# Stick-breaking attention: the causal mask inside the running product, and contiguous state transfers

## The chip, the cores and the metric

One core of one Trainium2 chip runs the whole step. The metric is the device time of one execution in microseconds; the median of several executions is compared. The profile is of one execution, recorded by the hardware. Its five engines are called here PE (TensorE, with its weight loads as PEld), DVE (VectorE), ACT (ScalarE), POOL (GpSimd) and SP (SyncE, which issues nearly all transfers).

## The reference

One inference step of a two-layer decoder, for 256 prompt rows and 8 sample rows (264 columns in all) that share the weights. Layer 0 mixes block-sparse attention with a gated unit, layer 1 mixes stick-breaking attention with a causal pooling mixer; each layer ends in a gated feed-forward net with a width-3 causal convolution. The change concerns layer 1:

```python
z = jnp.einsum('bqhd,bkhd->bhqk', qh, k).astype(jnp.float32) * scale
before = kpos[None, :] < pos[:, None]
log_keep = jnp.where(before, jax.nn.log_sigmoid(-z), 0.0)
later = lax.cumsum(log_keep, axis=3, reverse=True) - log_keep
w = jnp.where(before, jnp.exp(jax.nn.log_sigmoid(z) + later), 0.0)
return jnp.einsum('bhqk,bkhd->bqhd', w.astype(v.dtype), v)
```

So w is sigmoid(z) times the product of sigmoid(-z) over the later keys that come before the query, and zero from the query's own key on. The pooling mixer takes sums over windows of 2, 4, 8 and 16 rows; each sample brings its last 15 rows as state and hands back the last 15 of the new 16. The feed-forward net brings and hands back two state rows for each sample and layer in the same way.

## The kernel before

Activations lie transposed: features on the 128 partitions, the 264 rows along the free dimension. Every weight matrix is cut into 128x128 blocks, streamed in the order of use: a chunk `raw` of 16 blocks (1 MB) is loaded by SP into one of three buffers, tiles of 8 blocks are split into a high half `wh` (ACT, L300) and a low half `wl` (DVE, L301), and PE does three matmuls per block (L325 to L327). `split` runs three tiles ahead, so the DVE split of a chunk's second half is what frees its buffer for the chunk three later.

`run` goes through one phase (in0, out0, ff0, dn0, in1, out1, ff1, dn1) block by block. Between blocks it calls hooks: `blk(b, f)` puts a piece of attention or pooling work behind block b. In the phases in and out the order of PE's instructions is kept as written. A helper, `late`, issues a transfer on SP and keeps it at the place in SP's order where it was written; a plain `nc.sync.dma_start` may be moved by the scheduler. SP works strictly in order, so a transfer that waits holds up those behind it. The transfers on SP also share eight completion semaphores in turn, so each waits until the eighth before it has landed.

In the in1 phase of layer 1 the hooks are, in order: the pooling sums (`pool_sum`), the loads of the cached values V (two at every eighth block from 40), the pooling products `pm`, at 72 the sample scores (`zs_score`), from 80 on four groups `z_qk(t)` for the prompt (two heads each), at 82 the transposes pP of the samples' result (`zs_tr`), the transposes pt of the groups (`z_tr`), and at 100 and 108 the two groups of products with V, `pv_l`, which need all V loads of their samples.

A group `z_qk(t)` first writes a mask of -1e30 above and on the diagonal into both PSUM banks with a bf16 matmul of the identity and `maskb1` (L971), then adds the products of q and k: columns 0 to 127 for the first 128 queries, columns 128 to 383 for the others. `stick` (L958) then takes sigmoid(-z) of all 384 columns as `keep` and sigmoid(z) as `w` on ACT, runs the products backwards over the keys with one scan on DVE (L964; `edge` holds a 1 at column 127 at which the product starts anew), and multiplies (L965). The same function serves the samples, without a mask.

Three transfers of state have short pieces: `PALL` takes the pooling state, 15 of every 16 values, 32 times on each partition (60 bytes a piece, 4096 pieces); `out_pools` stores it shifted by one, 4096 pieces again; the two stores `out_cs` take 8 values for each of 22 blocks on each partition (32 bytes, 2816 pieces each).

Of the kernel before, what the change touches and what calls it, by code (L numbers as in the profile page):

```python
# [9 lines left out]
F32 = mybir.dt.float32  # L10
F32R = mybir.dt.float32r
BF16 = mybir.dt.bfloat16
I32 = mybir.dt.int32
AF = mybir.ActivationFunctionType
ALU = mybir.AluOpType
# [3 lines left out]
P = 128  # L19
D = 1024  # L20
KD = D // P
SEQ = 256
NS = 8
T = SEQ + NS
HD = 64
NH = 8
PAST = 256
# [4 lines left out]
NF = DFF // P  # L32
# [11 lines left out]
NEG = -1e30  # L44
SCALE = HD ** -0.5
POOLW = (2, 4, 8, 16)
NST = 15
# [33 lines left out]
_NB = sum(len(o) for _, o in _PHASES)  # L81
# [68 lines left out]
_NVEC = _vec_layout()  # L150
# [3 lines left out]
def _consts():  # L154
    f = np.float32
    parts = []

    def add(name, a):
        full = np.zeros((P, a.shape[1]), f)
        full[: a.shape[0]] = a  # L160
        _CST[name] = (sum(x.shape[1] for x in parts), a.shape[1])
        parts.append(full)

    half = 8
    inv = (f(500000.0) ** (-(np.arange(half, dtype=f) * f(2.0) / f(16)))).astype(f)
    pos = np.concatenate([np.arange(SEQ), np.full(NS, PAST)]).astype(f)
    ang = (pos[None, :] * inv[:, None]).astype(f)
    c, s = np.cos(ang.astype(np.float64)).astype(f), np.sin(ang.astype(np.float64)).astype(f)
    C, S = np.ones((P, T), f), np.zeros((P, T), f)
    for b in (0, 64):  # L170
        C[b:b + 8], C[b + 8:b + 16] = c, c
        S[b:b + 8], S[b + 8:b + 16] = -s, s
    r = np.arange(P)
    global _ROPE
    _ROPE = np.ascontiguousarray(np.concatenate([C, S], 1))
    add("ident", np.eye(P, dtype=f))
    add("m0", np.where(r[None, :] > r[:, None], f(NEG), f(0)).astype(f))
    add("m1", np.where(r[None, :] >= r[:, None], f(NEG), f(0)).astype(f))
    g32, h32 = r // 32, r % 32
    used = (h32 < 2 * NS)[:, None]  # L180
    ts = np.arange(4 * NS)[None, :]
    add("sm", (used & (g32[:, None] == ts // NS) & (h32[:, None] // 2 == ts % NS)).astype(f))
    add("hs", (used & (h32[:, None] % 2 == r[None, :] // HD)).astype(f))
    add("icnt", np.concatenate([np.tile((f(1) / np.minimum(np.arange(16) + 1, w).astype(f))[None, :], (P, 1)) for w in POOLW], 1))
    return np.ascontiguousarray(np.concatenate(parts, 1))


_CST_ARR = _consts()

_INS = [  # L190
    ("w", ((_NB - 16) * P * P,)), ("xw", (P * (KD + 16 * P + KD * T),)), ("x", (P, KD * T)), ("vec", (P, _NVEC)), ("cst", _CST_ARR.shape), ("rope", (P, 2 * T)),
    ("kt0", (NPHYS, P, 512)), ("vp0", (NPHYS, P, 512)), ("kt1", (NPHYS, P, 512)), ("vp1", (NPHYS, P, 512)),
    ("cstate", (P, 2 * NF * 2 * NS)), ("pstate", (P, 4 * NS * NST)),
    ("sguw", (P, 512)), ("sgub", (P, 512)), ("poolw", (P, 512)),
]
_OUTS = [
    ("y", (KD, P, T)), ("k0", (P, 4, T)), ("v0", (P, 4, T)), ("bvn", (P, 4, NS)),
    ("k1", (P, 4, T)), ("v1", (P, 4, T)), ("poolp", (P, 4, NST)), ("pools", (P, 4, NS, NST)),
    ("cv0", (P, NF, 10)), ("cv1", (P, NF, 10)), ("cs0", (P, NF, NS)), ("cs1", (P, NF, NS)),
]  # L200

# [2 lines left out]
def tile_decoder_step(ctx: ExitStack, tc: tile.TileContext, a):  # L204
    nc = tc.nc
    v, s, g = nc.vector, nc.scalar, nc.gpsimd
# [14 lines left out]
    pe = TensorE()  # L221

    con = ctx.enter_context(tc.tile_pool(name="con", bufs=1))
# [3 lines left out]
    pp = ctx.enter_context(tc.tile_pool(name="pp", bufs=4))  # L227
# [4 lines left out]
    def f4(name, shape=(P, 4, T), dt=F32):  # L232
        return up.tile(list(shape), dt, tag="u", name=name)
# [11 lines left out]
    VEC = con.tile([P, _NVEC], F32, name="VEC")  # L245
    CST = con.tile([P, _CST_ARR.shape[1]], F32, name="CST")
    PT = con.tile([1, NS * NPG], I32, name="PT")
    CSTATE = con.tile([P, 2, NF, 2, NS], F32, name="CSTATE")
    C0 = con.tile([P, 2, NF, NS], F32, name="C0")
    PALL = con.tile([P, 4, NS, 16], F32, name="PALL")  # L250

# [8 lines left out]
    def cst(n):  # L260
        o, w = _CST[n]
        return CST[:, o:o + w]
# [11 lines left out]
    def late(dst, src):  # L274
        tc.keep_in_program_order(nc.sync.dma_start(dst, src))
# [69 lines left out]
    first, o = [], 0  # L345
    for i in range(len(_FIRST)):
        g_, w_, x_ = _first_cols(i)
        n = g_ + w_ + x_
        r = f4(f"xw{i}", (P, n))
# [181 lines left out]
    def conv_prep(l):  # L531
        cw = vec("cw")
        w = lambda i: cw[:, (l * 3 + i) * NF:(l * 3 + i + 1) * NF].unsqueeze(2).to_broadcast([P, NF, NS])
        t = sm.tile([P, NF, NS], F32, tag="cprep", name=f"cprep{l}", bufs=1)
        g.tensor_tensor(C0[:, l], CSTATE[:, l, :, 0, :], w(0), ALU.mult)
        g.tensor_tensor(t, CSTATE[:, l, :, 1, :], w(1), ALU.mult)
        g.tensor_tensor(C0[:, l], C0[:, l], t, ALU.add)
        nc.sync.dma_start(a[f"cs{l}"], CSTATE[:, l, :, 1, :])

    def ffn(l, xg, R, down_evac, hooks=None):  # L540
        cw, cb = vec("cw"), vec("cb")
# [106 lines left out]
    rope = f4("rope")  # L648
# [9 lines left out]
            in0_evac(m, o)  # L658

    maskb0 = con.tile([P, 384], BF16, name="maskb0")  # L660
    maskb1 = con.tile([P, 384], BF16, name="maskb1")
    identb = con.tile([P, P], BF16, name="identb")

    def two(x):

        return x.rearrange("p (b k) -> p b k", k=P)[:, 0:3:2, :]

    def masks():
        for mk, c in ((maskb0, "m0"), (maskb1, "m1")):
            for b in (0, SEQ):  # L670
                tc.keep_in_program_order(s.activation(mk[:, b:b + P], cst(c), AF.Copy))
        tc.keep_in_program_order(s.activation(identb, ident, AF.Copy))

    q4, k4, v4 = f4("q4"), f4("k4"), f4("v4")
# [187 lines left out]
    blk = lambda b, f, *x: hk.at(b / 8 - 1, f, *x)  # L862
# [51 lines left out]
        blk(8, s_av, t)  # L914


    late(CSTATE, a["cstate"].rearrange("p (l j i s) -> p l j i s", l=2, j=NF, i=2))
    for l in range(2):
        conv_prep(l)

# [11 lines left out]
    ffn(0, xg, R, evac, hk)  # L932


    late(PALL[:, :, :, 0:NST], a["pstate"].rearrange("p (g s i) -> p g s i", g=4, s=NS))
    xg = xg1
    q4, k4, v4 = f4("q4b"), f4("k4b"), f4("v4b")
    vt = f4("vt1", (P, 2, 512))
# [9 lines left out]
    def norm1():  # L948
        nonlocal R
        R = nrm1.finish()  # L950
        sigmoid_set()


    edge = f4("edge", (P, 384))
    g.memset(edge, 0.0)
    g.memset(edge[:, P - 1:P], 1.0)

    def stick(w, z, n, e, name):  # L958


        keep = pp.tile([P, n], F32, tag="keep", name=f"keep_{name}", bufs=2)
        s.activation(keep, z, AF.Sigmoid, scale=-1.0)
        s.activation(w, z, AF.Sigmoid)
        v.tensor_tensor_scan(keep[:, ::-1], keep[:, ::-1], e[:, ::-1], 1.0, ALU.mult, ALU.max)  # L964
        v.tensor_tensor(w[:, :n - 1], w[:, :n - 1], keep[:, 1:], ALU.mult)  # L965

    def z_qk(t):
        pss = [at(f"Z1_{2 * t + i}") for i in range(2)]
        hd = [(q4[b:b + 64, t, :], k4[b:b + 64, t, :]) for b in (0, 64)]
        for ps in pss:  # L970
            pe.matmul(two(ps), identb, two(maskb1), start=True, stop=False, skip_group_check=True)  # L971
        for ps, (qh, kh) in zip(pss, hd):
            pe.matmul(ps[:, 0:P], qh[:, 0:P], kh[:, 0:P], start=False, stop=False, skip_group_check=True)
        for ps, (qh, kh) in zip(pss, hd):
            pe.matmul(ps[:, P:384], qh[:, P:SEQ], kh[:, 0:SEQ], start=False, stop=True, skip_group_check=True)
        for i, ps in enumerate(pss):
            w = st1["w", 2 * t + i] = pp.tile([P, 384], F32, tag="p", name=f"w1_{2 * t + i}")
            stick(w, ps[:, :384], 384, edge, 2 * t + i)
        if t == 3:
            lnexp()  # L980

# [14 lines left out]
    def zs_score():  # L996
        ps = at("sc1")
        sample_score(ps, sample_q(qz1, q4, v.tensor_copy), ktiles, range(NS))
        w = st1["zs"] = pp.tile([P, PAST], F32, tag="p", name="zs")
        stick(w, ps[:, :PAST], PAST, edge[:, P:], "s")  # L1000

    def zs_tr():
        pP = mmb("pP1")
# [65 lines left out]
        blk(b, z_qk, t)  # L1069
    for t, b in enumerate((91, 104, 116)):  # L1070
        blk(b, z_tr, t)
    blk(100, lambda: nc.sync.dma_start(a["k1"], k4))
    for i, b in enumerate((62, 66, 70, 76)):
        blk(b, pool_mix, i)
    for t, b in enumerate((110, 118, 126)):
# [1 line left out]
    for i, b in enumerate((100, 108)):  # L1077
        blk(b, sample_av_of(st1, PZ, vtiles, i, "l1"))
    run(orders["in1"], pick(xg), in1_evac, hk)
    nc.sync.dma_start(a["v1"], v4)  # L1080
    hk = Hooks()
    blk(1, zs_out)
    blk(2, z_tr, 3)
    blk(6, lambda: v_pair(vt, v4[:, 3, :], 3, "v1"))
    for t in range(4):
        blk(9, z_av, t)
    nc.sync.dma_start(a["poolp"], plp)
    nc.sync.dma_start(a["pools"], PALL[:, :, :, 1:16])

    xg, nrm, evac = residual(vec("f1"), "f1")  # L1090
    run(orders["out1"], pick([catA, catB]), evac, hk)
# [6 lines left out]
    for i, (m, e) in enumerate(YD):  # L1098
        x = X[:, m:e, :]
# [4 lines left out]
def _lay(inp):  # L1104
# [14 lines left out]
        "vec": np.concatenate([vecs[n] for n in _VEC], 1),  # L1119
        "cst": _CST_ARR,  # L1120
        "rope": _ROPE,
        "kt0": kt(f["cache_l0_kv"]), "vp0": f["cache_l0_kv"][:, :, 1].reshape(NPHYS, P, 512),
        "kt1": kt(f["cache_l1_kv"]), "vp1": f["cache_l1_kv"][:, :, 1].reshape(NPHYS, P, 512),
        "pt": f["page_table"].reshape(1, NS * NPG),
        "cstate": f["state_ffn_conv"].reshape(2, NS, 2, NF, P).transpose(4, 0, 3, 2, 1).reshape(P, -1),
        "pstate": f["state_l1_pool"].reshape(NS, NST, 4, P).transpose(3, 2, 0, 1).reshape(P, -1),
        "sguw": f["l0_sgu_w"].transpose(2, 0, 1).reshape(P, 512),
        "sgub": np.tile(f["l0_sgu_b"].reshape(1, 512), (P, 1)),
        "poolw": f["l1_pool_w"].transpose(1, 0, 2).reshape(P, 512),
# [40 lines left out]
```

## Time and profile before

| | us |
|---|---|
| median of three executions | 611.6 (610.9 to 612.25) |
| profiled execution, its own time | 612.44 |
| its span, first to last instruction | 610.3 |
| PE busy in the span | 593.2 (97%) |
| DVE / ACT / POOL busy | 417.4 / 343.8 / 66.7 |
| mean granted PE clock | 0.994 of full speed |

The span is what the profile shows; 2.14 us of the execution lie around it. Matmuls overlap in the pipeline: a single one is recorded with 284 ns, but they start 0.12 us apart, so their pace is read from stretches and not from single lengths. "a <- b" in a wait means that a stood still until b was done.

### The profile page before, as it was taken

How to read it: one execution, taken by the hardware profiler on the slowest of the kernel's cores; microseconds unless marked ns; L12 is line 12 of the kernel's file. 1: busy time of each engine (PE TensorE's matmuls, PEld its weight loads, DVE VectorE, ACT ScalarE, POOL GpSimd, SP SyncE). 2: the span in 40 equal slices, each digit the busy share in tenths (PEclk: the TensorE clock that was granted, in tenths of full speed). 3: DMA queues.
4: the chain of work that ended last, by engine and by line, in shares of the span. 5: the costliest groups of instructions: out<-in, count | busy, mean ns of one | idle time of the engine just before them, and what ended most of it. 6: DMA issues, size and time to landing. Idle time of an engine off the chain costs nothing.

```text
span 610.3 us, 12279 instructions
## 1 busy us (share of the span) xinstructions
PE 593.2 (97%) x4908; PEld 573.3 (94%) x4908; DVE 417.4 (68%) x711; ACT 343.8 (56%) x607; POOL 66.7 (11%) x83
## 2 busy tenths in 40 slices
PE   8999999999999999999999799999999999999994
PEld 7988879999999999999999588999999999999994
DVE  6899566879776766655559276597986766754442
ACT  7757755576655555544454256566665555555441
POOL 4100002341000000011110000033300000001120
PEclk9999999999999999999999999999999999999998
DMA  8998936544654554894579992445365454564502
GB/s 324 347 396 293 333 123 173 200 147 139 213 202 164 182 205 150 333 333 166 201 178 86 262 356 106 169 154 198 133 214 177 169 207 158 189 209 154 199 1 71
DMA packets 41258, 122.23 MB, mean 200 GB/s; under 512 B 17138, under 2 KB 18546, under 8 KB 29810
## 3 DMA queue, kind: packets, MB, share of 16 engines
q1 hardware_dynamic: 40368, 120.25, 60.0%
q10 hardware_dynamic: 834, 1.20, 0.6%
q8 instruction: 38, 0.62, 0.4%
q14 instruction: 18, 0.15, 0.1%
HBM read 117.50 MB, written 3.94 MB: 199 GB/s over the span
## 4 chain that ended last, share of the span: by engine, by line
PE 71%; DVE 3%; DMA 2%; issue 1%; ACT 1%; POOL 0%; DVEq 0%; SPq 0%; ACTq 0%
PE mm L216 68%; DMA raw<-in_w 2%; DVE xn_l L386 1%; DVE wl L301 1%; PE pv_l L216 1%; PE Z L216 1%; PE pav L216 0%; DVE wk L565 0%; PE pt L219 0%; DVE X L1100 0%; DVE wk L566 0%; ACT wh L300 0%; POOL wk L576 0%; DVE wk L561 0%; PE vtp_v L219 0%
## 5 line engine op out<-in xcount | busy, mean ns | idle before, releaser
L301 DVE TENSOR_TENSOR wl<-raw,wh 128x1024 fp32r<-128x1024 f32 x179 | 220.4, 1231 | 132.7 <-ACT wh L300 130.8
L300 ACT ACTIVATE wh<-raw 128x1024 fp32r<-128x1024 f32 x179 | 189.6, 1060 | 184.4 <-PE mm L216 164.0
L216 PE MATMUL mm<-xn_h,wh 128*128 128x264 f32 x544 | 154.7, 284 | 0.0
L216 PE MATMUL mm<-xn_l,wh 128*128 128x264 f32 x544 | 154.5, 284 | 0.0
L216 PE MATMUL mm<-xn_h,wl 128*128 128x264 f32 x544 | 153.4, 282 | 0.0
L216 PEld LDWEIGHTS mm<-xn_h,wh 128*128 128x128 f32 x544 | 102.2, 188 | 0.2 <-ACT cvo L568 0.2
L216 PEld LDWEIGHTS mm<-xn_l,wh 128*128 128x128 f32 x544 | 102.2, 188 | 0.0
L216 PEld LDWEIGHTS mm<-xn_h,wl 128*128 128x128 f32 x544 | 102.2, 188 | 0.0
L216 PE MATMUL mm<-a_l,wh 128*128 128x264 f32 x352 | 99.8, 284 | 0.0
L216 PE MATMUL mm<-a_h,wh 128*128 128x264 f32 x352 | 99.7, 284 | 0.0
L216 PE MATMUL mm<-a_h,wl 128*128 128x264 f32 x352 | 99.3, 282 | 0.0
L216 PEld LDWEIGHTS mm<-a_l,wh 128*128 128x128 f32 x352 | 66.1, 188 | 0.0
L216 PEld LDWEIGHTS mm<-a_h,wl 128*128 128x128 f32 x352 | 66.1, 188 | 0.0
L216 PEld LDWEIGHTS mm<-a_h,wh 128*128 128x128 f32 x352 | 66.0, 188 | 0.0
L216 PE MATMUL mm<-xg_h,wh 128*128 128x264 f32 x160 | 48.2, 301 | 1.3 <-ACT xg_h L385 1.3
L216 PE MATMUL mm<-xg_f_h,wh 128*128 128x264 f32 x160 | 46.0, 288 | 2.0 <-DVE wk L575 2.0
L216 PE MATMUL mm<-xg_l,wh 128*128 128x264 f32 x160 | 46.2, 289 | 0.0
L216 PE MATMUL mm<-xg_h,wl 128*128 128x264 f32 x160 | 46.1, 288 | 0.0
L216 PE MATMUL mm<-xg_f_l,wh 128*128 128x264 f32 x160 | 45.4, 284 | 0.0
L216 PE MATMUL mm<-xg_f_h,wl 128*128 128x264 f32 x160 | 45.1, 282 | 0.0
L216 PE MATMUL mm<-xg_n_h,wh 128*128 128x264 f32 x128 | 39.2, 307 | 0.0
L216 PE MATMUL mm<-xg_n_l,wh 128*128 128x264 f32 x128 | 36.9, 288 | 0.0
(249 smaller groups left out, 1055.5 us busy)
## 6 DMA issues: line engine op xcount, KB each, us to landing
raw<-in_w SPq DMA_DIRECT2D x89, 1024.0 KB, 4.9
K<-in_kt SPq DMA_DIRECT2D x32, 256.0 KB, 6.1
V<-in_vp SPq DMA_DIRECT2D x32, 256.0 KB, 7.2
raw<-in_w SPq DMA_DIRECT2D x4, 512.0 KB, 5.8
X<-in_x SPq DMA_DIRECT2D x4, 264.0 KB
xw<-in_xw SPq DMA_DIRECT2D x2, 388.0 KB, 5.6
out_k<-k SPq DMA_DIRECT2D x1, 528.0 KB
out_v<-v SPq DMA_DIRECT2D x1, 528.0 KB
```

What stands on the lines that cost most here:

```text
L216: return self.keep(nc.tensor.matmul(*x, **k))
L300: s.activation(h, src, AF.Copy)
L301: v.tensor_tensor(l, src, h.bitcast(F32), ALU.subtract)
L386: j = v.scalar_tensor_tensor(l, src, gain, h.bitcast(F32), ALU.mult, ALU.subtract)
```

## The change

The mask products and `maskb1` go. The first Z product now starts the bank. `keep` moves to two fixed tiles of 385 columns, in which columns 128 and 384 hold zero; ACT fills columns 1 to 127 and 129 to 383 in two instructions. The scan runs over columns 383 to 1 from 0, and `edge`, now an input loaded by SP, has a 1 at each row's own key, the first that is masked: as the scan takes the larger of the product and the edge, it stays zero beyond that key and starts with 1 there. The samples get a function of their own, `stick_all`, with one zero column of `edge` broadcast.

PALL is loaded and stored in full, 16 of 16 values (the first is dropped on the host), and CSTATE is laid out so that its load and the stores `out_cs` are one piece per row. The stores of the pooling state, k1 and v1 are written with `late` at blocks 84, 112 and (in out1) 12.

```diff
+    _EDGE = np.zeros((P, 384), f)
+    _EDGE[r[1:], r[1:]], _EDGE[r, 2 * P + r] = 1, 1
...
-    add("m1", np.where(r[None, :] >= r[:, None], f(NEG), f(0)).astype(f))
...
-    ("cstate", (P, 2 * NF * 2 * NS)), ("pstate", (P, 4 * NS * NST)),
+    ("cstate", (P, 2 * NF * 2 * NS)), ("pstate", (P, 4 * NS * 16)),
...
-    CSTATE = con.tile([P, 2, NF, 2, NS], F32, name="CSTATE")
+    CSTATE = con.tile([P, 2, 2, NF, NS], F32, name="CSTATE")
...
-        nc.sync.dma_start(a[f"cs{l}"], CSTATE[:, l, :, 1, :])
+        nc.sync.dma_start(a[f"cs{l}"], CSTATE[:, l, 1])
...
-        for mk, c in ((maskb0, "m0"), (maskb1, "m1")):
-            for b in (0, SEQ):
-                tc.keep_in_program_order(s.activation(mk[:, b:b + P], cst(c), AF.Copy))
+        for b in (0, SEQ):
+            tc.keep_in_program_order(s.activation(maskb0[:, b:b + P], cst("m0"), AF.Copy))
...
-    late(PALL[:, :, :, 0:NST], a["pstate"].rearrange("p (g s i) -> p g s i", g=4, s=NS))
+    late(PALL, a["pstate"].rearrange("p (g s i) -> p g s i", g=4, s=NS))
...
     edge = f4("edge", (P, 384))
-    g.memset(edge, 0.0)
-    g.memset(edge[:, P - 1:P], 1.0)
-
-    def stick(w, z, n, e, name):
-        keep = pp.tile([P, n], F32, tag="keep", name=f"keep_{name}", bufs=2)
+    late(edge, a["edge"])
+
+    keeps = [con.tile([P, 385], F32, name=f"keep{i}") for i in range(2)]
+    for z in keeps:
+        g.memset(z[:, P:P + 1], 0.0)
+        g.memset(z[:, 384:385], 0.0)
+
+    def stick(w, z, t):
+        n, keep = 384, keeps[t % 2]
+        for a0, a1 in ((1, P), (P + 1, n)):
+            s.activation(keep[:, a0:a1], z[:, a0:a1], AF.Sigmoid, scale=-1.0)
+        s.activation(w, z, AF.Sigmoid)
+        v.tensor_tensor_scan(keep[:, 1:n][:, ::-1], keep[:, 1:n][:, ::-1], edge[:, 1:][:, ::-1], 0.0, ALU.mult, ALU.max)
+        v.tensor_tensor(w, w, keep[:, 1:], ALU.mult)
+
+    def stick_all(w, z):
+        n = PAST
+        keep = pp.tile([P, n], F32, tag="p", name="keep_s")
         s.activation(keep, z, AF.Sigmoid, scale=-1.0)
         s.activation(w, z, AF.Sigmoid)
-        v.tensor_tensor_scan(keep[:, ::-1], keep[:, ::-1], e[:, ::-1], 1.0, ALU.mult, ALU.max)
+        v.tensor_tensor_scan(keep[:, ::-1], keep[:, ::-1], edge[:, P:P + 1].to_broadcast([P, n]), 1.0, ALU.mult, ALU.max)
         v.tensor_tensor(w[:, :n - 1], w[:, :n - 1], keep[:, 1:], ALU.mult)
...
-        for ps in pss:
-            pe.matmul(two(ps), identb, two(maskb1), start=True, stop=False, skip_group_check=True)
         for ps, (qh, kh) in zip(pss, hd):
-            pe.matmul(ps[:, 0:P], qh[:, 0:P], kh[:, 0:P], start=False, stop=False, skip_group_check=True)
+            pe.matmul(ps[:, 0:P], qh[:, 0:P], kh[:, 0:P], start=True, stop=False, skip_group_check=True)
...
-    blk(100, lambda: nc.sync.dma_start(a["k1"], k4))
+    blk(84, late, a["poolp"], plp)
+    blk(84, late, a["pools"], PALL)
+    blk(112, late, a["k1"], k4)
...
-    nc.sync.dma_start(a["v1"], v4)
...
-    nc.sync.dma_start(a["poolp"], plp)
-    nc.sync.dma_start(a["pools"], PALL[:, :, :, 1:16])
+    blk(12, late, a["v1"], v4)
```

More of the change, by code (lines that the diff above doesn't have):

```diff
@@ L173, in _consts @@
     r = np.arange(P)
-    global _ROPE
+    global _ROPE, _EDGE
+    _EDGE = np.zeros((P, 384), f)
+    _EDGE[r[1:], r[1:]], _EDGE[r, 2 * P + r] = 1, 1
     _ROPE = np.ascontiguousarray(np.concatenate([C, S], 1))
@@ L190 @@
 _INS = [
-    ("w", ((_NB - 16) * P * P,)), ("xw", (P * (KD + 16 * P + KD * T),)), ("x", (P, KD * T)), ("vec", (P, _NVEC)), ("cst", _CST_ARR.shape), ("rope", (P, 2 * T)),
+    ("w", ((_NB - 16) * P * P,)), ("xw", (P * (KD + 16 * P + KD * T),)), ("x", (P, KD * T)), ("vec", (P, _NVEC)), ("cst", _CST_ARR.shape), ("rope", (P, 2 * T)), ("edge", (P, 384)),
     ("kt0", (NPHYS, P, 512)), ("vp0", (NPHYS, P, 512)), ("kt1", (NPHYS, P, 512)), ("vp1", (NPHYS, P, 512)),
-    ("cstate", (P, 2 * NF * 2 * NS)), ("pstate", (P, 4 * NS * NST)),
+    ("cstate", (P, 2 * NF * 2 * NS)), ("pstate", (P, 4 * NS * 16)),
     ("sguw", (P, 512)), ("sgub", (P, 512)), ("poolw", (P, 512)),
@@ L197 @@
     ("y", (KD, P, T)), ("k0", (P, 4, T)), ("v0", (P, 4, T)), ("bvn", (P, 4, NS)),
-    ("k1", (P, 4, T)), ("v1", (P, 4, T)), ("poolp", (P, 4, NST)), ("pools", (P, 4, NS, NST)),
+    ("k1", (P, 4, T)), ("v1", (P, 4, T)), ("poolp", (P, 4, NST)), ("pools", (P, 4, NS, 16)),
     ("cv0", (P, NF, 10)), ("cv1", (P, NF, 10)), ("cs0", (P, NF, NS)), ("cs1", (P, NF, NS)),
@@ L534, in conv_prep @@
         t = sm.tile([P, NF, NS], F32, tag="cprep", name=f"cprep{l}", bufs=1)
-        g.tensor_tensor(C0[:, l], CSTATE[:, l, :, 0, :], w(0), ALU.mult)
-        g.tensor_tensor(t, CSTATE[:, l, :, 1, :], w(1), ALU.mult)
+        g.tensor_tensor(C0[:, l], CSTATE[:, l, 0], w(0), ALU.mult)
+        g.tensor_tensor(t, CSTATE[:, l, 1], w(1), ALU.mult)
         g.tensor_tensor(C0[:, l], C0[:, l], t, ALU.add)
-        nc.sync.dma_start(a[f"cs{l}"], CSTATE[:, l, :, 1, :])
+        nc.sync.dma_start(a[f"cs{l}"], CSTATE[:, l, 1])
     def ffn(l, xg, R, down_evac, hooks=None):
@@ L660, in tile_decoder_step @@
     maskb0 = con.tile([P, 384], BF16, name="maskb0")
-    maskb1 = con.tile([P, 384], BF16, name="maskb1")
     identb = con.tile([P, P], BF16, name="identb")
@@ L914, in tile_decoder_step @@
         blk(8, s_av, t)
-    late(CSTATE, a["cstate"].rearrange("p (l j i s) -> p l j i s", l=2, j=NF, i=2))
+    late(CSTATE, a["cstate"].rearrange("p (l i j s) -> p l i j s", l=2, i=2, j=NF))
     for l in range(2):
@@ L977, in z_qk @@
             w = st1["w", 2 * t + i] = pp.tile([P, 384], F32, tag="p", name=f"w1_{2 * t + i}")
-            stick(w, ps[:, :384], 384, edge, 2 * t + i)
+            stick(w, ps[:, :384], 2 * t + i)
         if t == 3:
@@ L999, in zs_score @@
         w = st1["zs"] = pp.tile([P, PAST], F32, tag="p", name="zs")
-        stick(w, ps[:, :PAST], PAST, edge[:, P:], "s")
+        stick_all(w, ps[:, :PAST])
     def zs_tr():
@@ L1121, in _lay @@
         "rope": _ROPE,
+        "edge": _EDGE,
         "kt0": kt(f["cache_l0_kv"]), "vp0": f["cache_l0_kv"][:, :, 1].reshape(NPHYS, P, 512),
@@ L1124, in _lay @@
         "pt": f["page_table"].reshape(1, NS * NPG),
-        "cstate": f["state_ffn_conv"].reshape(2, NS, 2, NF, P).transpose(4, 0, 3, 2, 1).reshape(P, -1),
-        "pstate": f["state_l1_pool"].reshape(NS, NST, 4, P).transpose(3, 2, 0, 1).reshape(P, -1),
+        "cstate": f["state_ffn_conv"].reshape(2, NS, 2, NF, P).transpose(4, 0, 2, 3, 1).reshape(P, -1),
+        "pstate": np.pad(f["state_l1_pool"].reshape(NS, NST, 4, P).transpose(3, 2, 0, 1), ((0, 0), (0, 0), (0, 0), (0, 1))).reshape(P, -1),
         "sguw": f["l0_sgu_w"].transpose(2, 0, 1).reshape(P, 512),
@@ L1160 @@
     poolp = o["poolp"].transpose(2, 1, 0).reshape(1, NST, 512)
-    pools = o["pools"].transpose(2, 3, 1, 0).reshape(NS, NST, 512)
+    pools = o["pools"][..., 1:].transpose(2, 3, 1, 0).reshape(NS, NST, 512)
     cvp, cvs = [], []
```

## The prediction

> **What bounds the kernel now.** I read the page first, then the windows, the chain that ended last, the waits, and the SyncE queue's timeline around the one place where TensorE stands still.
>
> ```profile
> span 610.3 us, 12279 instructions
> ...
> PE 593.2 (97%) x4908; PEld 573.3 (94%) x4908; DVE 417.4 (68%) x711; ACT 343.8 (56%) x607; POOL 66.7 (11%) x83
> ...
> DMA packets 41258, 122.23 MB, mean 200 GB/s; under 512 B 17138, under 2 KB 18546, under 8 KB 29810
> ```
>
> TensorE is busy for 593.2 of 610.3 us, so an edit can pay in two ways only: by taking matmuls away, or by closing one of the gaps that make up the other 17.1 us. In windows of 2 us (PE busy, PEld, DVE, ACT, POOL, granted clock, DMA share, GB/s) the largest gap stands out:
>
> ```profile
> 330.00:332.00 2.00, 2.00 (x19) 2.00 (x18) 2.00 (x8) 1.07 (x1) 0.00 (x0) 1.00 1.57 20
> ...
> 348.00:350.00 2.00, 0.00 (x0) 0.00 (x0) 1.71 (x2) 2.00 (x5) 0.00 (x0) 1.00 0.97 406
> 350.00:352.00 2.00, 1.30 (x6) 1.30 (x7) 1.90 (x5) 1.88 (x7) 0.00 (x0) 0.60 1.03 391
> 352.00:354.00 2.00, 2.00 (x12) 2.00 (x11) 2.00 (x3) 0.00 (x0) 0.00 (x0) 0.55 1.10 434
> ```
>
> TensorE does nothing from 348 to 350, and after that the granted clock is 0.60 and 0.55. The chain that ended last (start, length, what) and the waits say why:
>
> ```profile
> 333.64 13.46 DMA raw<-in_w
> ...
> 347.20 1.07 ACT wh L300
> ...
> 350.22 0.44 DVE zs L965
> ...
> 350.70 0.69 PE pP L219 x2
> 351.39 4.41 PE mm L216 x27
> ...
> 357.18 1.09 PE Z L216 x10
> ...
> 370.69 0.22 PE vtp_v L219 x2
> ...
> 387.70 25.27 PE mm L216 x207
> ```
> ```profile
> ACT wh L300 <- DMA raw<-in_w: 14.1, 2, 9.7
> ...
> PE pP L219 <- DVE zs L965: 3.9, 1, 3.9
> ```
>
> One weight chunk was issued at 333.64 and landed at 347.10. ScalarE waited 9.7 us for it with the sample scores' sigmoids queued behind, and TensorE, whose order is fixed, waited 3.9 us at the transposes pP. Why 13.46 us for a chunk?
>
> ```profile
> 306.62 0.64 SPq L275 DMA_DIRECT2D PALL<-in_pstate  x1
> 307.31 4.75 SPq L275 DMA_DIRECT2D pw<-in_poolw  x1
> ...
> 322.37 0.58 SPq L1088 DMA_DIRECT2D out_pools<-PALL  x1
> 323.01 7.76 SPq L1087 DMA_DIRECT2D out_poolp<-plp  x1
> ...
> 333.64 0.42 SPq L275 DMA_DIRECT2D raw<-in_w  x1
> ```
> ```profile
> raw<-in_w SPq DMA_DIRECT2D x89, 1024.0 KB, 4.9
> ```
> ```profile
> 341.98 0.33 SPq L275 DMA_DIRECT2D V<-in_vp  x1
> ```
> ```profile
> SPq L275 <- DMA out_pools<-PALL: 5.1, 1, 5.1
> ```
>
> The median chunk lands in 4.9 us. Ahead of this one stands the pool-state store, 4096 pieces of 60 bytes, issued at 322.37. The 30 KB store behind it needs 7.76 us only to be issued, and the V load at 341.98 still waits 5.1 us for the big store: it took 341.98 - 322.37 = 19.6 us. Meanwhile the engines moved 20 GB/s at a share of 1.57. The load of PALL (also 4096 pieces) did the same to the issue behind it, 4.75 us.
>
> **The change part by part.**
>
> *States in one piece, stores moved (the larger part).* PALL's load and the pools store become 128 pieces of 2 KB each. In the built program the two pool stores move from ahead of the first V load to behind the sixth pair (V10), and k1 and v1 each go one chunk later; nothing else moves on SyncE. So V0 follows chunk 55 at once, and the late chunk (56) then has one gate left: the split of its predecessor's second half, which frees the buffer.
>
> ```profile
> 323.84 1.21 DVE L301 TENSOR_TENSOR wl<-raw,wh 128x1024 fp32r<-128x1024 f32 x1
> ```
>
> That split ends at 325.05, so the chunk can be issued 8.6 us earlier than at 333.64. With the median 4.9 us it lands at 330; with the old 13.46 us even then at 338.5. It is needed when? TensorE ran dry because zs came at 350.66; from landing to zs the chain took 350.66 - 347.10 = 3.56 us, and zs is needed at 350.70 - 3.9 = 346.8. So any landing before 343.2 closes the gap, and both values do. What goes with the gap:
> - the wait itself, 3.89 us (3.9 in the row);
> - the slow clock after it: 27 matmuls took 4.41 us, at the pace of the 207 (25.27 / 207 = 0.122) they take 3.30, so 1.11; the two pP transposes 0.69 against 0.22 for two alike (vtp_v), so 0.47.
>
> Together 5.47 us.
>
> *The mask products.* Eight bf16 matmuls (two ahead of each of four Z groups) go, with eight weight loads.
>
> ```profile
> 344.63 0.39 PE L216 MATMUL Z<-maskb,identb 128*128 128x256 bf16 x2
> 344.96 0.93 PE L216 MATMUL Z<-k4b,q4b 64*128 64x128 f32 x8
> ```
> ```profile
> 360.73 0.28 PE L216 MATMUL mm<-xg_n_h,wl 128*128 128x264 f32 x1
> 360.94 0.64 PE L216 MATMUL pv_l<-V,PZ 128*32 128x512 f32 x4
> ```
>
> From the mask's start to the first product 0.33 us. Without masks Z follows a projection matmul directly; a projection matmul's own pace is 0.12 (the 207 above), but the step from one to the fp32 pv is 0.21 (360.73 to 360.94). So each group gives back 0.24 to 0.33; I take 0.28, which is 1.1 us for four (0.95 to 1.3). TensorE is the bound here, so this counts in full.
>
> *ScalarE in the sticks.* Each 384-wide keep becomes a 127- and a 255-wide one, eight more instructions; two casts of the old mask go.
>
> ```profile
> L962 ACT ACTIVATE keep<-Z 128x384 f32<-128x384 f32 x8 | 4.0, 498 | 2.6 <-PE Z L216 1.3 <-issue 1.3
> ...
> L671 ACT ACTIVATE maskb<-CST 128x128 bf16<-128x128 f32 x4 | 0.9, 296 | 0.0
> ...
> L962 ACT ACTIVATE keep_s<-sc 128x256 f32<-128x256 f32 x1 | 0.4, 366 | 0.0
> ```
>
> 296 + 366 - 498 = 0.16 us more per head as an upper bound, 0.33 per pair. By the Trainium skill, "ScalarE: Activation LUTs", section What ACT_TABLE_LOAD costs, a split adds 186 ns less an overlap of 93, an estimate of 0.09 per head and 0.19 per pair; no row here has the 127-wide form. Does anything wait for it?
>
> ```profile
> 361.60 0.55 DVE L965 TENSOR_TENSOR w<-w,keep 128x383 f32<-128x383 f32 x1
> ...
> 364.23 0.68 PEld L219 LDWEIGHTS pt<-CST,w 128*128 128x128 f32 x6
> ```
>
> In the second group the last w is ready at 362.15, 3.9 us after Z ended (358.27), and 2.1 us before its transposes: covered. In the first group the cover is thinner once the gap is closed. There six matmuls, pP and 27 matmuls lie between Z and the transposes, 33 x 0.122 + 0.22 = 4.25 us, against 3.9 plus 0.33. I cost it at nothing, up to 0.5 if the split of a weight tile falls in between. The scan keeps its length (383 for 384) and its place.
>
> *The edge load* replaces two memsets on GpSimd and puts 192 KB between pw and chunk 54.
>
> ```profile
> 304.80 0.42 POOL L955 MEMSET edge<- 128x384 f32 x1
> ```
>
> The memset, which waits for the same buffer, ran at 304.80, so the load does not wait when SyncE comes to it after 307.3; it costs an issue of about 0.4 (as the chunk at 333.64) while pw behind PALL loses its 4.75. Nothing.
>
> *CSTATE.* The two cs stores go from 2816 pieces of 32 bytes to 128 of 704.
>
> ```profile
> 100.00:131.00 31.00, 31.00 (x257) 30.93 (x256) 24.41 (x32) 19.71 (x33) 10.79 (x12) 1.00 0.54 200
> ```
>
> They lie in a stretch where TensorE never pauses: nothing. The same goes for the smaller constants and four one-column memsets at the start.
>
> **The sum.** 5.47 + 1.1 = 6.6 us. The profiled execution took 612.44 (610.3 of span, 2.14 around it), which gives 605.9; it stood 0.84 above the median of 611.6, so the median becomes 605.0.
>
> **The rivals.**
>
> *A wait is left in the first group* (chance 0.10). The thin cover above does not hold, or chunk 56 still comes a little late, and TensorE waits 0.5 to 2 us. With 1 us: 606.0, and no clock is lost if a short wait leaves it alone. The Trainium skill, "TensorE: Matmul & The Clock Gate", section Part 1: The HAM clock gate, halves the clock only after an idle window of about 3.4 us; the trace's 3.9 us fits that, and no row here shows where between short and 3.9 it begins.
>
> *The stall stays* (0.07). If it is not the 60-byte pieces but plain bytes (16 V loads and the chunks, 406 and 434 GB/s in the windows), chunk 56 stays late and only the masks pay: 611.6 - 1.1 = 610.5. [...]
>
> *Slower* (0.05). The pool stores now stand inside the V stream, and in the built program each transfer waits for the landing of the eighth before it. If V14 comes late, the second pv group waits.
>
> ```profile
> L275 SPq DMA_DIRECT2D V<-in_vp x16: 332/333/1785, 331.0 to 355.0; - x16
> ...
> DMA to landing us min/median/max: 7.1/9.0/13.5
> ```
> ```profile
> 367.83 0.16 PEld L216 LDWEIGHTS pv_l<-V,PZ 128*32 128x32 f32 x8
> ```
>
> TensorE would come there at 367.83 - 5.47 - 0.56 = 361.8. If V14 is issued at 355.0 as now and takes the longest 13.5, it lands at 368.5: a wait of 6.7 and 1.6 of clock, 605.0 + 8.3 = 613.3. It decides from a landing at 366.8, where 5.0 of wait and 1.6 of clock give back the 6.6. Against it: V0 stands where the stores stood, from 322.37 on, so the V stream starts 8 us or more before its 331.0.
>
> **How the numbers follow.** The forecast has 0.78, the rivals 0.10, 0.07 and 0.05. This kernel's measurement tells about 0.2%, 1.2 us, from no change; faster is the forecast and the first rival, 0.88, same the second, 0.07, slower 0.05. Low end: masks 1.3 and the run-to-run 0.7 of the times shown, 604.1. High end: the masks' lower bound, 0.5 in the first group and the first rival to 2 us, 607.2.
>
> **What would show it.** Right: chunk 56 issued near 325 and landed before 343, no wait of pP for zs, clock 1.00 through 350 to 354, the first Z product about 0.2 after the projection matmul, TensorE busy near 593.2 - 1.58 - 1.1 = 590.5 us in a span near 603.7, under 512-byte packets down by over 13,000. Wrong: a raw landing still near 347, a wait of TensorE at pt or pv_l of over 1 us, or an SP issue blocked for several us.

## The result, and the profile after

The changed kernel takes 605.19 us (median of 4 runs, 604.84 to 605.91) and the kernel before, run beside it, 611.92 (4 runs, 610.9 to 613.54): ratio 0.9889, 95% interval 0.9865 to 0.9913. The forecast was 605.0. The profiled execution took 605.24 us, 603.5 of it span.

The page of the kernel after, the lines that answer to those of before:

```profile
span 603.5 us, 12273 instructions
...
PE 591.0 (98%) x4900; PEld 572.0 (95%) x4900; DVE 417.6 (69%) x711; ACT 344.4 (57%) x613; POOL 67.5 (11%) x85
...
DMA packets 28090, 122.39 MB, mean 203 GB/s; under 512 B 3330, under 2 KB 5250, under 8 KB 16642
```

TensorE's idle time (span less busy) fell from 17.1 to 12.5 us, its busy time by 2.2, and 13,808 packets of under 512 bytes are gone. The windows of 2 us of the kernel after (columns as before) at the place of the gap:

```profile
330.00:332.00 2.00, 2.00 (x18) 2.00 (x17) 2.00 (x6) 0.82 (x1) 0.00 (x0) 1.00 1.06 372
...
348.00:350.00 2.00, 2.00 (x19) 2.00 (x18) 2.00 (x5) 1.30 (x2) 0.00 (x0) 1.00 0.95 367
350.00:352.00 2.00, 2.00 (x18) 1.53 (x17) 0.54 (x1) 0.91 (x4) 0.00 (x0) 1.00 0.96 374
352.00:354.00 2.00, 2.00 (x19) 2.00 (x18) 1.59 (x3) 2.00 (x6) 0.00 (x0) 1.00 0.09 36
```

TensorE is busy without a pause at a granted clock of 1.00, and at 330 the engines move 372 GB/s where they moved 20. SyncE's queue in the kernel after (start, length until the issue is done):

```profile
306.74 0.42 SPq L277 DMA_DIRECT2D pw<-in_poolw  x1
307.20 0.53 SPq L277 DMA_DIRECT2D edge<-in_edge  x1
...
324.39 0.34 SPq L277 DMA_DIRECT2D raw<-in_w  x1
...
341.59 0.44 SPq L277 DMA_DIRECT2D out_pools<-PALL  x1
...
346.96 0.86 SPq L277 DMA_DIRECT2D V<-in_vp  x2
```

No issue is blocked for several us any more: pw behind PALL takes 0.42 us for 4.75, and the late chunk (56) goes out at 324.39 for 333.64 and lands in 4.8 us for 13.46. The chain of work that ended last (start, length, what) has no DMA in this stretch:

```profile
313.40 0.45 PE ns_n L218 x2
...
344.11 0.86 PE Z L218 x8
344.97 0.93 PE mm L218 x6
345.90 0.22 PE pP L221 x2
346.12 3.28 PE mm L218 x27
349.40 0.66 PE pt L221 x6
...
598.12 1.58 DVE X L1111 x3
```

The transposes pP follow their matmuls at once and take 0.22 us for 0.69; the 27 matmuls behind them 3.28 for 4.41; a Z group 0.86 for 1.09. Of TensorE's waits the chunk's is gone and none is at Z, pt or pv_l; the longest that are left are short ones in other stages:

```profile
PE warm L218 <- DVE warm L373: 1.2, 1, 1.2
PE mm L218 <- DVE wk L577: 1.0, 1, 1.0
```

One distance is used below to compare traces: from the start of ns_n (the sums of layer 1's first norm) to the start of the last X piece, both in the chain. In the kernel before it has these ends:

```profile
314.09 0.45 PE ns_n L216 x2
...
605.22 1.58 DVE X L1100 x3
```

It was 291.13 us there and is 598.12 - 313.40 = 284.72 after: 6.41 less. The span fell by 6.8: 0.7 of that lies ahead of ns_n, and the end behind the last X piece became about 0.25 longer.

### The profile page after: what moved, and what is told of

The parts are those of the page before. It is cut to its first block, busy times and chain, and to the rows that moved or that the text cites. A ratio compares the mean times of both kernels' runs of the same rounds, so it can differ in the third digit from the quotient of the medians.

```text
span 603.5 us, 12273 instructions
## 1 busy us (share of the span) xinstructions
PE 591.0 (98%) x4900; PEld 572.0 (95%) x4900; DVE 417.6 (69%) x711; ACT 344.4 (57%) x613; POOL 67.5 (11%) x85
## 4 chain that ended last, share of the span: by engine, by line
PE 73%; DVE 3%; ACT 1%; issue 1%; POOL 0%; DVEq 0%; ACTq 0%
PE mm L218 70%; DVE xn_l L388 1%; PE pv_l L218 1%; PE sc L218 1%; PE Z L218 1%; PE pav L218 0%; DVE wk L567 0%; PE pt L221 0%; DVE wl L303 0%; DVE X L1111 0%; PE pm L218 0%; ACT wh L302 0%; POOL wk L578 0%; DVE wk L563 0%; DVE wk L568 0%
```

## The experiments

The theory: short pieces in SyncE's queue made the gap. The main rivals: the place of the stores did it, or the bytes; or the mask part pays more than its Z groups show.

**The state part alone** (e1_states: the kernel before with the new state layout, CSTATE's too, and the new place of the stores, k1 and v1 among them; masks and sticks as before).

```diff
-    late(PALL[:, :, :, 0:NST], a["pstate"]...)
+    late(PALL, a["pstate"]...)
...
+    blk(84, late, a["poolp"], plp)
+    blk(84, late, a["pools"], PALL)
...
-    nc.sync.dma_start(a["pools"], PALL[:, :, :, 1:16])
...
```

> The kernel before with the state part of the change alone (states and their stores in one piece per row, stores in the written order); masks, edge and stick as before. Theory A (the gap came from the 60-byte pieces in SyncE's queue): the wait at pP goes, 0 instead of 3.9 us, clock 1.00 after it, and the time is 5.5 us under the kernel before, about 606.2. Theory C (the gap was a matter of bytes, and the mask part closed it): the wait stays and the time is within 0.5 us of before.

Measured: 606.91 us (606.69 to 607.51, 4 runs) beside 611.57, ratio 0.9928 (0.9904 to 0.9952). There is no wait at pP, and the chunk went out at 325.69. The state part brings most of the gain.

**The mask part alone** (e2_mask: the changed kernel with the state part undone).

```diff
-    late(PALL, a["pstate"]...)
+    late(PALL[:, :, :, 0:NST], a["pstate"]...)
...
-    blk(84, late, a["pools"], PALL)
...
+    nc.sync.dma_start(a["pools"], PALL[:, :, :, 1:16])
...
```

> The changed kernel with the state part undone (short pieces, old stores); masks in the running product as changed. Theory A: the wait at pP stays at 3 to 4 us with its slow clock, only the mask products are saved, four times 0.23 = 0.9 us (groups of Z from 1.09 to 0.86 us), time 0.7 to 1.3 us under before. Theory C: the wait shrinks and the time falls by over 3 us.

Measured: 610.94 us (12 runs) beside 611.57, ratio 0.9999 (0.9985 to 1.0013). The gap is there again, by the waits and by the chain:

```profile
PE pP L221 <- DVE zs L978: 3.5, 1, 3.5
```
```profile
330.46 14.82 DMA raw<-in_w
...
348.88 0.44 PE pP L221 x2
349.32 4.81 PE mm L218 x27
```

The distance is 289.95, 5.23 more than in the kernel after: 3.5 of wait, 0.22 at pP and 1.53 at the 27 matmuls. Against the kernel before it is 1.18 less, of which 0.4 is the shorter wait; the medians differ by 0.63, under the 0.7 that was expected, and the ratio does not leave 1: so small a part does not show in the time of this kernel, whose clock varies (below).

**Pieces or place?** The kernel before, once with only the place of the stores changed, k1 and v1 included (e3_order) and once with only PALL's load and store in one piece per row (e4_pieces).

```diff
 e3_order
+    blk(84, late, a["poolp"], plp)
+    blk(84, late, a["pools"], PALL[:, :, :, 1:16])
...
-    nc.sync.dma_start(a["poolp"], plp)
-    nc.sync.dma_start(a["pools"], PALL[:, :, :, 1:16])
...
 e4_pieces
-    late(PALL[:, :, :, 0:NST], a["pstate"]...)
+    late(PALL, a["pstate"]...)
...
-    nc.sync.dma_start(a["pools"], PALL[:, :, :, 1:16])
+    nc.sync.dma_start(a["pools"], PALL)
...
```

> The kernel before with only the place of the stores changed (pooling stores behind V10, k1 and v1 one chunk later); all pieces as short as before. Theory A (pieces): the chunk that was late gets ahead of the store, so the wait at pP goes, but the store's 4096 pieces now hold up V12, V14 and the chunk behind them: an issue on SyncE blocked for 5 to 8 us near 342, V14 landing 10 to 20 us later than in the changed kernel, and a new wait of 0 to 4 us at the second pv_l group; time 606 to 611. Theory B (place alone decides): as the state part in full, about 606.2, with nothing late.

> The kernel before with the pooling state loaded and stored in one piece per row, and nothing else: the stores stay in their old place ahead of V0, CSTATE as before. Theory A (pieces): no issue is blocked, the chunk lands in 5 to 7 us, the wait at pP goes, about 606.2. Theory B (place): the wait at pP stays above 2 us and the time above 609.

The new place with short pieces: 612.9 us (10 runs), ratio 1.0033 (1.0015 to 1.0051), so slower by 0.3%. The waits, the queue and the chain of e3_order:

```profile
PE pv_l L216 <- DMA V<-in_vp: 3.1, 1, 3.1
```
```profile
341.10 1.68 SPq L275 DMA_DIRECT2D out_pools<-PALL  x1
...
343.03 13.14 SPq L275 DMA_DIRECT2D V<-in_vp  x2
```
```profile
356.90 9.38 DMA V<-in_vp
...
366.32 3.44 PE pv_l L216 x10
```

The wait at pP went, and another came: behind the store in its new place the next pair of V loads takes 13.14 us to be issued, the pair after it goes out only at 356.90 (346.96 in the kernel after) and lands at 366.28, and the second pv group waits and then runs at a slow clock (10 matmuls 3.44 us, where 16 take 1.85 in the kernel after). The distance is 291.42, 0.29 above the kernel before: one gap was exchanged for another.

The old place with long pieces: 606.64 us (606.18 to 607.5, 4 runs), ratio 0.9928 (0.9903 to 0.9953). The queue of e4_pieces:

```profile
321.98 0.34 SPq L1088 DMA_DIRECT2D out_pools<-PALL  x1
322.37 0.42 SPq L1087 DMA_DIRECT2D out_poolp<-plp  x1
325.00 0.42 SPq L275 DMA_DIRECT2D raw<-in_w  x1
```

The store behind the big one takes 0.42 us to issue for 7.76, and the distance is 285.59, 5.54 less than before. So the pieces made the gap; with long pieces the place is worth nothing that is seen here, and with short ones it harms.

**Which of the two, load or store?** The kernel before with only the load (e5_load) or only the store (e5_store) in one piece.

```diff
 e5_load
-    late(PALL[:, :, :, 0:NST], a["pstate"]...)
+    late(PALL, a["pstate"]...)
...
 e5_store
-    nc.sync.dma_start(a["pools"], PALL[:, :, :, 1:16])
+    nc.sync.dma_start(a["pools"], PALL)
...
```

> The kernel before with only the load of the pooling state in one piece per row; its store stays in 4096 pieces of 60 bytes. If the store makes the gap: the issue of pw is no longer held (0.4 instead of 4.75 us), but the wait at pP stays at 3 to 4 us and the time within 0.5 us of before. If load and store fill the queue together: the wait falls below 2 us and the time by over 2 us.

> The kernel before with only the store of the pooling state in one piece per row; its load stays in 4096 pieces. If the store makes the gap: the wait at pP goes and the time is 5.0 to 5.6 us under before, as with both in one piece. If load and store fill the queue together: a wait of 1 to 2 us stays.

The store alone brings all of it: 606.75 us (10 runs) beside 610.06, ratio 0.9945 (0.9925 to 0.9964), distance 285.62, although pw is still blocked behind PALL in the queue of e5_store:

```profile
307.23 4.47 SPq L275 DMA_DIRECT2D pw<-in_poolw  x1
...
322.51 0.42 SPq L1087 DMA_DIRECT2D out_poolp<-plp  x1
324.93 0.42 SPq L275 DMA_DIRECT2D raw<-in_w  x1
```

The load alone was a surprise: 607.99 us (10 runs), ratio 0.9962 (0.9942 to 0.9982), distance 287.09, most of the gain too. The waits, the queue and the chain of e5_load:

```profile
PE pP L219 <- DVE zs L965: 0.5, 1, 0.5
```
```profile
323.07 6.55 SPq L1087 DMA_DIRECT2D out_poolp<-plp  x1
```
```profile
331.06 12.74 DMA raw<-in_w
```

The store still blocks the queue (6.55 us), but the chunk is issued at 331.06 for 333.64 and lands at 343.80 for 347.10, and TensorE waits 0.5 us at pP, with 0.4 more at pt. This is the edge of the gap: the prediction had put the landing that just does at 343.2. Why a load 16 us ahead still matters for the store is open; no run separates its pieces from those of the store inside the queue. Part of the shift may be no more than a difference between executions: from the store's issue to the chunk's it was 11.27 us in the kernel before and 8.61 here, but 9.30 in e2_mask, where load and store are both short (the store landed in 19.6, 16.4 and 18.2 us).

**How long must a wait be to cost the clock?** The first rival assumed that a wait of up to 2 us costs no clock. The changed kernel, with multiplications by one on GpSimd ahead of pP that make it wait (e8_wait_short has six, e9_wait_long eight).

```diff
     def zs_tr():
+        for _ in range(6):
+            g.tensor_tensor(st1["zs"], st1["zs"], ones[:, 0:1].to_broadcast([P, PAST]), ALU.mult)
```

> The changed kernel with six GpSimd multiplications by one put between zs and its transposes pP, about 1.0 us each, so that TensorE waits there again, for about 2.5 us. If the clock is lost only after a longer idle stretch: granted clock 1.00 after it, time 2.5 us over the changed kernel. If every wait of microseconds costs clock: 0.5 to 1.6 us more, and windows with a clock under 0.9.

> The same with eight multiplications: TensorE waits about 4.5 us. The prediction's sum put 1.58 us of lost clock behind a wait of 3.89: so two windows near 0.55 after the wait, and 6.1 us over the changed kernel. If the slow clock behind the old gap had another cause: 4.5 us over the changed kernel and clock 1.00.

e8_wait_short took 609.0 us (10 runs, ratio 0.9971, 0.9951 to 0.9992, to the kernel before). Its wait, its windows and its chain:

```profile
PE pP L221 <- POOL zs L1015: 2.2, 1, 2.2
```
```profile
348.00:350.00 2.00, 1.89 (x11) 1.89 (x12) 1.79 (x3) 0.34 (x2) 0.06 (x1) 0.64 1.04 382
350.00:352.00 2.00, 2.00 (x11) 2.00 (x11) 0.00 (x0) 0.00 (x0) 0.00 (x0) 0.50 0.92 370
```
```profile
348.55 4.81 PE mm L218 x27
```

The clock was lost behind a wait of 2.2 us in the profiled execution: the 27 matmuls took 4.81 us for 3.28, pP 0.44 for 0.22, and the distance is 288.64, 3.92 more than in the kernel after. Two of the ten executions took 606.96 and 606.97 us at a mean clock of 0.997, the other eight 608.51 to 610.55 at 0.992 to 0.995. So the same edit costs about 2 or about 4 us; no trace of the two was kept, so how long they waited is not shown.

e9_wait_long took 612.49 us (10 runs, ratio 1.0034, 1.0015 to 1.0054). Its wait, its windows and its chain:

```profile
PE pP L221 <- POOL zs L1015: 4.3, 1, 4.3
```
```profile
350.00:352.00 2.00, 1.39 (x8) 1.39 (x9) 0.97 (x2) 0.34 (x2) 0.56 (x1) 0.77 0.99 407
352.00:354.00 2.00, 2.00 (x11) 2.00 (x10) 0.00 (x0) 0.00 (x0) 0.00 (x0) 0.50 0.44 167
354.00:356.00 2.00, 2.00 (x17) 2.00 (x16) 0.66 (x2) 1.06 (x1) 0.00 (x0) 0.88 0.03 8
```
```profile
351.05 4.82 PE mm L218 x27
```

The distance is 290.76, 6.04 more than after: 4.30 of wait and the same 1.74 of clock. The gap of the kernel before, put back by other means, brings the distance back to within 0.4 of its 291.13. The median lies 2.4 us above the 610.06 of the kernel before on that chip, whose executions were faster than the profiled one (below).

**The mask part by its time.** The changed kernel and the state part alone, once more and on one chip, so that the mask part is the only difference. The edits are nil and that of e1_states.

> The changed kernel once more, on one chip with the state part alone (the next run), so that the mask part is the only difference between the two. Theory: the mask part is worth what the Z groups of the traces give, 4 x 0.23 = 0.9 us of median; the prediction's term was 1.1. Rival: the smaller Z groups are given back at a later wait, and the medians lie within 0.3 us of each other. Against the kernel before: 605.2, ratio about 0.989.

> The state part alone once more (one piece per row and the new place of the stores; masks and sticks as in the kernel before). Theory: 0.9 us above the changed kernel on the same chip, near 606.2, with 8 Z-group matmuls more and Z groups of 1.09 us for 0.86. Rival: within 0.3 us of it.

605.54 us (605.08 to 606.1, 6 runs) against 606.9 (605.96 to 609.76, 12 runs): 1.4 us between the medians. Beside 609.74 of the kernel before the ratios are 0.9925 (0.9904 to 0.9947), where 0.989 was expected, and 0.995 (0.9933 to 0.9968). The chains, first of e10_both, then of e11_states_again:

```profile
344.23 0.86 PE Z L218 x8
```
```profile
343.80 1.09 PE Z L216 x10
```

The Z group gives back 0.23 us, and the distances, 284.71 and 285.66, differ by 0.95, four times that. The rival of a later wait is out. The span differs by 0.3 only (603.6 and 603.9): the end behind the last X piece is 0.2 longer with the mask part, and the start ahead of ns_n was 0.4 longer in this execution. The time around the span is about 0.35 us shorter with it (below), so that the two profiled executions are 0.6 apart.

## Why the prediction was right, point by point

**The gap.** Every link held: the chunk issued at 324.39 (near 325 forecast), no wait at pP, the clock 1.00 through 350 to 354. 3.89 + 1.58 = 5.47 us were forecast; e4_pieces, which changes only the pieces, shows 5.54 and e5_store 5.51. The cause was argued from a queue's blocked issues, and the runs now show it. A chunk's median landing stayed 4.9 us:

```profile
raw<-in_w SPq DMA_DIRECT2D x89, 1024.0 KB, 4.9
...
out_pools<-PALL SPq DMA_DIRECT2D x1, 256.0 KB, 5.7
```

The store itself lands in 5.7 us for 19.6, with more bytes. The Trainium skill, "DMA: Bandwidth & Descriptors", section Anatomy of one DMA, fits about 2.0 us plus the bytes at 436 GB/s to transfers issued by GpSimd, an estimate of 2.6 us for as many bytes. This store goes by SyncE: the row of long pieces is twice that among the V loads, the row of short ones seven times.

**The mask products.** The term was 1.1 us (0.95 to 1.3) and measured 4 x 0.23 = 0.92, just below its range. The step that was off is the choice of 0.28 between 0.24 and 0.33 where a row was nearer to one end. In the timeline of the kernel after the first Z product starts 0.21 us behind the last projection matmul, exactly the step that the prediction read at pv_l and then averaged away:

```profile
343.83 0.28 PE L218 MATMUL mm<-xg_n_h,wl 128*128 128x264 f32 x1
344.04 0.93 PE L218 MATMUL Z<-k4b,q4b 64*128 64x128 f32 x8
```

**A term that was left out.** The end behind the last X piece (from its start to the end of the span) was about 5.1 us in the seven traces without the mask part, the kernel before among them, and about 5.3 in the five with it. Behind the last issues of out_y the timeline shows no instruction; what the 0.25 us are stays open. They are not lost in the time, though: an execution was longer than its span by 2.06 to 2.23 us in every run without the mask part and by 1.74 to 1.91 in every run with it, some 0.35 less. The prediction took the 2.14 us around the span as fixed. The two together give back nothing of the 0.92.

**ScalarE in the sticks.** Costed at nothing under a thin cover, and the cover held, by little. The timeline of the kernel after:

```profile
347.97 1.00 DVE L969 TENSOR_TENSOR w<-w,keep 128x384 f32<-128x384 f32 x2
...
349.12 0.69 PEld L221 LDWEIGHTS pt<-CST,w 128*128 128x128 f32 x6
```

The last w of the first group is ready at 348.97, 0.15 us ahead of its transposes. From the start of a keep to that of its w, ScalarE takes 0.42 to 0.43 us with the two pieces, where it took 0.37 to 0.39 with the one in the kernel before: about 0.05 more per head. By the Trainium skill, "ScalarE: Activation LUTs", section What ACT_TABLE_LOAD costs, the estimate was 0.09; the bound from rows was 0.16.

**Edge load and CSTATE.** Nothing, as forecast: the edge load's issue took 0.53 us in a queue that waited for nobody there, and the distances of e10_both, which has it, and e11_states_again, which has not, differ by 0.95, which the 0.92 of the mask products explain. CSTATE's transfers lie ahead of ns_n, where the distance does not reach; from the span's start to ns_n it was 313.09 to 314.71 us in the six traces with the new CSTATE and 312.88 to 314.17 in the six with the old.

**The sum.** 6.6 us were forecast for the profiled execution and 6.4 came between ns_n and the last X piece. The rest of the 7.2 us between the two profiled executions lies outside the sum: 0.7 us at the start-up, and 0.35 around the span less the 0.25 at its end. The start-up's was this execution's: TensorE's wait for DVE's k ahead of ns_n was 0.9 us in the kernel before and 0.3 after, but between nothing and 1.6 in the other runs, with and without the change.

**The rivals.** *A wait is left* did not come, and its price was wrong. It rested on no clock being lost behind a wait of 1 to 2 us; e8_wait_short shows 1.7 us lost behind 2.2 in its trace, and by the times and mean clocks in eight executions of ten, so a wait of 2 us could have cost 2 or 4. The Trainium skill, "TensorE: Matmul & The Clock Gate", section Part 1: The HAM clock gate, names an idle window of about 3.4 us before the clock halves; the 2.2 us of this run are shorter, and the run decides. *The stall stays* fell with e4_pieces: the bytes grew and the stall went. *Slower* has a real mechanism that e3_order shows at the place named, a V load late for the second pv group, with its clock behind it (3.1 us of wait, V landed at 366.28); it needs the short pieces, which the change takes away in the same step. The prediction priced the two parts of that step together and so was safe; the place alone is a loss.

**How firm the size is.** The kernel before had medians of 609.74 to 611.92 us in the sets of runs shown, its executions mean clocks of 0.989 to 0.998. The changed kernel gave 605.19 and 605.54. The ratio was 0.9889 once and 0.9925 once, with intervals that overlap; the change is faster in both. The forecast was worked out from one profiled execution of 612.44 us, above all these medians. Between medians the change brought 6.7 us in the first set and 4.2 in the second, and the pieces alone 4.9 (e4_pieces) and 3.3 (e5_store), where the traces show 5.5. So it is in part luck that 605.19 came so near to 605.0. Of the 71 executions of the kernel before that ran beside the experiments, 31 had a mean clock of 0.996 or more, with medians of 609.4 to 609.9 us in the three sets; the other 40 had medians of 610.5 to 611.9. Probably the slow clock behind the gap is not paid in every execution, but no trace of one that was spared was kept.

## What to carry to other kernels

Look at what an issue costs on its queue, not only at how long its transfer takes: a 30 KB store that needs 7.76 us to be issued says that the transfer ahead is cut into too many pieces, and the one who pays may be a load for another engine 20 us later. Lengthen the pieces before moving the transfer: the move alone only chose another victim. Price a stall of TensorE as the wait and the slow clock behind it, and where two rows bracket a cost, take the one whose neighbours are alike rather than the middle.

## What was not expected of the hardware

The clock cost behind a stall hardly depends on its length: 1.6 us behind 3.9 (the kernel before), 1.75 behind 3.5, 1.73 behind 2.2 and 1.74 behind 4.3, and none behind 0.5 and 0.4 (e5_load), each in one trace. The windows show the same: what they lack to a clock of 1.00 adds up to 2 x (0.40 + 0.45) = 1.70 us in the kernel before, to 2 x (0.36 + 0.50) = 1.72 in e8_wait_short and to 2 x (0.23 + 0.50 + 0.12) = 1.70 in e9_wait_long. In the record of the granted clock that these traces hold, and those of e2_mask and e3_order, the slow stretch is one of 3.41 us at 0.50, however long the wait was; in the kernel before it began 0.3 us ahead of the wait's end, which is why only 1.6 was paid there.

It also begins at fixed steps. From the first rise of the clock to the slow stretch it is 100 times 3.413 us in the kernel before, e2_mask and e9_wait_long, 99 times in e8_wait_short and 104 times in e3_order. The first rise itself came between 4.4 and 11.6 us into the span in the twelve traces. So whether a wait of about 2 us loses the clock may depend on how it falls on these steps. That would fit the two executions of e8_wait_short that did not pay; it is not shown.

And with the load of 4096 short pieces in one piece per row, the issue of a chunk some 20 us later came 2.6 us earlier and the time fell by 2 us (e5_load against the kernel before); by what, is open.
